# Attention values with 256 moving columns: the parity of the key block picks the column half of the array, and the two partial sums are added afterwards

## The chip, the cores and the metric

One Trainium2 chip, one of its cores. The metric is the device time of one execution in microseconds (us); the median of three executions of the kernel before is 1148.51 us.

## The reference, cut to what matters

One layer of a transformer trunk for 640 tokens (128 context tokens and 512 latent tokens), width 1024: a norm with modulation, a combined projection, grouped attention beside a short gated convolution, a merge, and a feed-forward part. The change lies in the last step of the attention, the product of the probabilities with the values:

```python
def one_block(qblk):
    s = jnp.einsum('bqkgd,btkd->bkgqt', qblk, k).astype(jnp.float32) * scale
    p = jax.nn.softmax(s, axis=-1).astype(v.dtype)
    return jnp.einsum('bkgqt,btkd->bqkgd', p, v)
```

There are 16 query heads of 64 columns and 4 heads of keys and values, so four query heads share one head of keys and values; call these four a **group** g (0 to 3). Latent queries see 640 keys (512 latent, 128 cached), context queries see the 128 context keys. All data are 32-bit floats.

## The kernel before, in words

The program has three long stages: a prologue with the projections of keys and values, the attention (about 75 to 298 us of the profiled span), and then a row of large products that run to the end. The first product after the attention is the attention's output projection.

**Attention.** For each group there are nine **steps**, i = 0 to 8. Step 0 treats the context queries; steps 1 to 8 treat one block of 128 latent queries and a pair of heads each. TensorE, ScalarE and VectorE run in exactly the order in which the code is written (a manual schedule); GpSimd's order is chosen by the scheduler. In one step:

- TensorE computes scores into two PSUM tiles `s` of a pool of three (12 matmuls, line 603). A score tile can be overwritten when the exponentials of the scores that it held are done.
- In steps 0, 3, 4, 5 and 8 TensorE also transposes a block of queries into the PSUM bank S1[1] (`s1b` in the profile, line 584), and multiplies a later block of queries into S1[0] (`s1a`, 24 matmuls of 256 columns at lines 161 to 163). In group 3, which has no next group, 24 matmuls of a gate (`gate_part`) into S1[0] stand there in steps 3, 4, 5 and 8. In steps 0, 1, 4 and 6 there are 32 small matmuls of the modulation (line 214).
- VectorE takes two row maxima (line 739), ScalarE makes the scale of each (741) and the exponentials with their sums (742), VectorE the reciprocal of the sums (745), GpSimd multiplies the probabilities by it, one head at a time (750), and VectorE transposes the result in 32 by 32 blocks into one of six slots of the SBUF tile PT (755), one step later. ScalarE and VectorE also make the high and low halves of a weight (700, 701) in steps 1 and 6, and VectorE and GpSimd rotate and scale the queries (538 to 558).

**The values** (class `Values`). PT holds transposed probabilities in blocks of 32 keys. A matmul takes 32 partitions of PT (one of four 32-row strips i, which are different queries) as moving data, and a block of 32 keys by 64 value columns as weights, so eight such matmuls work in eight tiles of the array at a time: four row strips by two column halves of 64. Before the change the column half is the head h of the pair: the same weights stand in both halves, and each half sees the 128 columns (4 slots by 32 queries) of its own head. Twenty key blocks are accumulated. Strip i writes to its own PSUM bank: strips 0 and 1 to the two banks of a tile `s`, strips 2 and 3 to S1[0] and S1[1]. Each 32-bit matmul appears as two matmuls and two weight loads in the profile.

One group needs two such sums, the **halves**: half 0 (three query blocks, the context block among them, which `own` adds with four key blocks) is spread over steps 6 and 7, half 1 (two query blocks) over steps 1 and 2 of the next group, and for group 3 after its last step. When the last matmul of a half is done, at the end of step 7 or 2, ScalarE copies the sums to the high tensor AH (three activations, line 796), and VectorE subtracts this from the sums into the low tensor AL (three instructions, line 800). Only then are S1[0], S1[1] and the tile `s` free: the transposition of queries in step 8 or 3 waits for S1[1], the query or gate product behind it for S1[0].

**The end of the attention.** After step 8 of group 3 TensorE runs 18 matmuls of 384 columns for a gate (`gate1`), four small ones that fold the modulation (line 240); VectorE finishes the modulation (244 to 247) and transposes the last probabilities (755); then the last half runs, with 6 more gate matmuls in it, and when its sums have been read from S1[0] and S1[1], the projection starts in banks `b` that take the place of S1.

Tile names in the profile: `s`, `s1a`, `s1b` are the PSUM tiles above, `AL`, `KH`, `KL` hold value blocks when they are inputs of line 783 (they are reused as room for the values of a group), `CT` the transposed context probabilities.

## Time and profile before

| | us |
|---|---|
| three executions | 1143.9, 1148.51, 1150.22 |
| the profiled execution's own time | 1150.66 |
| its span, first to last instruction | 1148.9 |
| attention from group 0's step 6 to group 3's step 6 | 152.38 |
| from there to the first matmul of the projection | 39.01 |
| matmuls in the program, as profiled | 10013 |

The span is what all views of the profile share out; the profiled execution's own time is 1.8 us longer, and lies 2.15 us above the median. In the profile "PE" is TensorE's matmuls, "PEld" its weight loads, DVE is VectorE, ACT is ScalarE, POOL is GpSimd. Each row of a timeline starts with the start and the duration in us; a bracket at the row's end says how long the engine sat idle before it, and what ended that. "issue" means that nothing the profile shows was waited for. In a table of windows, a row gives the window, its length, then for each engine its busy time and in parentheses its instructions, then the share of TensorE's clock that was granted.

### The profile page before, as it was taken

To read this page: it belongs to the slowest core of one execution; us is meant where nothing else is said; L and a number is where in the kernel's file an instruction comes from. 1 tells how busy PE (TensorE), PEld (TensorE's weight loads), DVE (VectorE), ACT (ScalarE), POOL (GpSimd) and SP (SyncE) were. 2 spreads that over 40 slices of the span, in tenths; PEclk is the share of its full clock that TensorE was granted. 3 is DMA by queue.
4 is the path that set the end of the run, shared out by engine and by line. 5 is a ranking of instruction groups with operands and counts; after the bars stand their busy time and mean duration, and the time that the engine had idled before them with its cause. 6 is when DMAs were issued, how large, how long until landed. Compare 5 with 4: busy or idle time off the path is not lost.

```text
span 1148.9 us, 23748 instructions
## 1 busy us (share of the span) xinstructions
PE 1100.1 (96%) x10013; PEld 1020.2 (89%) x10013; DVE 819.5 (71%) x1194; ACT 555.4 (48%) x999; POOL 162.2 (14%) x198
## 2 busy tenths in 40 slices
PE   7998888897999999999999999999999999999997
PEld 5787777787999999999999888999999999998786
DVE  5578777885454788898745447887887778888644
ACT  4375555564233545454532347555545455555431
POOL 2057564663000000000000012000000000002001
PEclk9998999998899999999999999999999999999999
DMA  9664336341122233233242543333333233315632
GB/s 336 205 171 148 113 94 140 94 130 57 45 70 73 74 97 88 74 94 90 74 127 75 185 165 126 92 115 101 103 115 96 93 102 106 113 60 184 229 106 91
DMA packets 189000, 133.65 MB, mean 116 GB/s; under 512 B 16914, under 2 KB 171086, under 8 KB 188878
## 3 DMA queue, kind: packets, MB, share of 16 engines
q1 hardware_dynamic: 188782, 132.11, 37.3%
q8 instruction: 78, 1.28, 0.5%
q14 instruction: 28, 0.23, 0.1%
q10 hardware_dynamic: 112, 0.04, 0.0%
HBM read 120.01 MB, written 12.24 MB: 115 GB/s over the span
## 4 chain that ended last, share of the span: by engine, by line
PE 90%; DVE 3%; issue 3%; DMA 2%; ACT 1%; SPq 1%; POOL 0%; DVEq 0%; POOLq 0%; ACTq 0%
PE b L1011 44%; PE b L163 9%; PE b L161 9%; PE b L162 9%; PE s L603 3%; PE s L783 3%; PE s1a L161 2%; PE s1a L162 2%; PE s1a L163 2%; DVE Y L1495 1%; PE s L161 1%; PE s1a L783 1%; PE s L163 1%; DMA XT<-in_w_ada_dram 1%; PE s L162 1%
## 5 line engine op out<-in xcount | busy, mean ns | idle before, releaser
L1011 PE MATMUL b<-ZB,whi 128*128 128x322 f32 x1024 | 228.6, 310 | 0.0
L1011 PEld LDWEIGHTS b<-ZB,whi 128*128 128x128 f32 x1024 | 173.8, 189 | 1.6
L1011 PE MATMUL b<-ZB,wlo 128*128 128x322 f32 x512 | 159.5, 311 | 0.0
L1011 PE MATMUL b<-MT,whi 128*128 128x320 f32 x608 | 134.2, 308 | 0.0
L1011 PEld LDWEIGHTS b<-MT,whi 128*128 128x128 f32 x608 | 101.6, 188 | 0.0
L1011 PEld LDWEIGHTS b<-ZB,wlo 128*128 128x128 f32 x512 | 96.3, 188 | 0.0
L750 POOL TENSOR_TENSOR pr<-pr,sm 128x640 f32<-128x640 f32 x64 | 86.7, 1375 | 57.7 <-DVE sm L745 56.9
L1011 PE MATMUL b<-MT,wlo 128*128 128x320 f32 x304 | 93.8, 309 | 0.0
L1495 DVE SCALAR_TENSOR_TENSOR Y<-C,cffn,Y 128x642 f32<-128x642 f32 x88 | 80.8, 920 | 0.9
L998 ACT ACTIVATE whi<-SUM 128x1024 fp32r<-128x1024 f32 x40 | 42.2, 1056 | 79.6 <-DVE SUM L1465 77.2
L136 DVE TENSOR_TENSOR wlo<-raw,whi 128x1024 fp32r<-128x1024 f32 (+1 forms) x31 | 33.7, 1086 | 52.6 <-ACT whi L135 52.1
L1011 PE MATMUL b<-UH,whi 128*128 128x320 f32 x228 | 70.6, 310 | 0.0
L1011 PE MATMUL b<-UL,whi 128*128 128x320 f32 x228 | 70.5, 309 | 0.0
L1011 PE MATMUL b<-UH,wlo 128*128 128x320 f32 x228 | 70.3, 308 | 0.0
L1002 DVE TENSOR_TENSOR wlo<-raw,whi 128x1024 fp32r<-128x1024 f32 (+1 forms) x51 | 50.4, 1020 | 25.2 <-ACT whi L998 24.4
L998 ACT ACTIVATE whi<-WB 128x1024 fp32r<-128x1024 f32 x38 | 40.1, 1055 | 54.9 <-DVE WB L1106 54.9
L1019 ACT ACTIVATE p<-b 128x322 f32<-128x322 f32 (+1 forms) x78 | 34.2, 439 | 58.3 <-PE b L1011 58.3
L742 ACT ACTIVATE pr<-s,mr,rq 128x640 f32<-128x640 f32 x64 | 56.6, 885 | 3.8
L1011 PEld LDWEIGHTS b<-MT,wlo 128*128 128x128 f32 x304 | 57.0, 188 | 0.0
L1022 DVE TENSOR_TENSOR C<-b,p 128x322 f32<-128x322 f32 x40 | 19.7, 492 | 52.3 <-PE b L1011 51.8
L739 DVE TENSOR_REDUCE mx<-s 128x1 f32<-128x640 f32 x64 | 49.6, 816 | 8.7 <-PE s L603 8.2
L1002 DVE TENSOR_TENSOR wlo<-WB,whi 128x1024 fp32r<-128x1024 f32 x38 | 46.5, 1223 | 8.5 <-ACT whi L998 8.5
(379 smaller groups left out, 3151.9 us busy)
## 6 DMA issues: line engine op xcount, KB each, us to landing
raw<-in_w_in_dram SPq DMA_DIRECT2D x48, 512.0 KB, 3.6
RAW<-in_w_up_dram SPq DMA_DIRECT2D x40, 512.0 KB, 3.9
raw<-in_w_ada_dram SPq DMA_DIRECT2D x32, 512.0 KB, 4.6
raw<-in_w_down_dram SPq DMA_DIRECT2D x22, 512.0 KB, 3.8
actd<-Y SPq DMA_DIRECT2D x18, 321.0 KB, 2.6
AFB<-actd SPq DMA_DIRECT2D x18, 321.0 KB, 4.5
XT<-in_w_ada_dram SPq DMA_DIRECT2D x9, 512.0 KB, 5.7
raw<-in_w_conv_out_dram SPq DMA_DIRECT2D x9, 512.0 KB, 4.1
```

What stands on the lines that cost most here:

```text
L161: PE.matmul(out, ah, bh, start=start, stop=False)
L162: PE.matmul(out, ah, bl, start=False, stop=False)
L163: PE.matmul(out, al, bh, start=False, stop=stop)
L603: PE.matmul(outs[h], q[rows, pi, :], kk[rows, g, ks], start=n == 0, stop=n == 2, tile_position=(64 * h, 0))
L739: V.tensor_reduce(out=mx, in_=self.sc[h], axis=AX.X, op=ALU.max, negate=True)
L742: S.activation(self.pr[:, h, :], self.sc[h], AF.Exp, bias=low, scale=rs, accum_out=self.sm[:, h:h + 1])
L750: G.tensor_tensor(out=self.pr[:, h, :], in0=self.pr[:, h, :], in1=self.sm[:, h:h + 1].broadcast_to((128, NTOK)), op=ALU.mult)
L783: PE.matmul(self.out(i, h, 64, 192), VR[self.g][rows, c, :], PT[rows, s0:s0 + 4, h, 32 * c:32 * c + 32], start=c == 0, stop=c == 19, tile_ ...
L998: S.activation(to[0], raw, AF.Copy)
L1002: V.tensor_tensor(out=lo, in0=raw, in1=hi.bitcast(F32), op=ALU.subtract)
L1011: PE.matmul(out, p[:, ws], q[:, k, :], start=start and k == 0 and n == 0, stop=stop and k == 3 and n == 2, skip_group_check=True)
L1495: V.scalar_tensor_tensor(out=y, in0=crows(j)[i][:, d:d + NACT], scalar=cffn[:, 44 * d + o:44 * d + o + 1], in1=y, op0=ALU.mult, op1=ALU.add)
```

## The change

The roles of the two column halves change. Both halves now see the same kind of moving data, the 256 columns of both heads (4 slots by 2 heads by 32 queries), and the half is picked by the parity of the key block: even blocks accumulate in PSUM partitions 0 to 63, odd blocks in partitions 64 to 127. Each half of a group takes ten pairs of blocks, and `own` two, so there are half as many matmuls (and weight loads) with twice the columns. What leaves the array are two partial sums that have to be added. The new method `sums` does this: ScalarE copies the odd partial sums from PSUM to SBUF (three activations, into slots of PT that have been used up), and VectorE adds even and odd in eight instructions over 64 partitions, and writes the complete sums into another part of these slots, head 0 to partitions 0 to 63 and head 1 to 64 to 127. `high` is then one activation from SBUF, and `low` one instruction, on GpSimd, except for the last half, where it is on VectorE. The output of a strip now takes 384 of the 512 columns of a bank (before 192), so the modulation's results in S1[1] move from columns 256 to 383 to columns 384 to 511. What each step computes, and the order of the steps, stay as they are; the parts of a half are divided alike (3 and 7 pairs for 6 and 14 blocks, 5 and 5 for 10 and 10; 3, 3, 4 pairs for 7, 7, 6 blocks at the end).

```diff
-                        for h in range(2):
-                            PE.matmul(self.out(i, h, 64, 192), VR[self.g][rows, c, :], PT[rows, s0:s0 + 4, h, 32 * c:32 * c + 32],
-                                      start=c == 0, stop=c == 19, tile_position=(32 * i, 64 * h))
+                        for c in (2 * n, 2 * n + 1):
+                            PE.matmul(self.out(i, c % 2, 128, 384), VR[self.g][rows, c, :], PT[rows, s0:s0 + 4, :, 32 * c:32 * c + 32],
+                                      start=n == 0, stop=n == 9, tile_position=(32 * i, 64 * (c % 2)))
...
+            def sums(self):
+                a, q = (128, 2) if self.half else (0, 3)
+                w, s0 = 384 - a, 4 if self.half else 0
+                room = PT[:, s0:s0 + 2].rearrange("p s h c -> p (s h c)")
+                odd = room[0:64, 0:4 * w].rearrange("p (i c) -> p i c", i=4)
+                self.all = room[:, 4 * w:6 * w].rearrange("p (k c) -> p k c", k=2)
+                dst = self.all.rearrange("p k (q i b) -> p i q k b", q=q, i=4)
+                both = self.p.rearrange("p (e c) -> p e c", e=2)[:, :, a:384]
+                for i in (1, 0):
+                    S.activation(odd[:, 2 + i], S1[i][64:128, a:384], AF.Copy)
+                S.activation(odd[:, 0:2], both[64:128], AF.Copy)
+                one, two = "p (q k h b) -> p h q k b", "p e (q k h b) -> p h q k e b"
+                for h in range(2):
+                    rows = slice(64 * h, 64 * h + 64)
+                    for i in (1, 0):
+                        x, y = (z.rearrange(one, h=2, k=2, b=32)[:, h] for z in (S1[i][0:64, a:384], odd[:, 2 + i]))
+                        V.tensor_tensor(out=dst[rows, 2 + i], in0=x, in1=y, op=ALU.add)
+                    for k in range(2):
+                        x, y = (z.rearrange(two, h=2, k=2, b=32)[:, h, :, k] for z in (both[0:64], odd[:, 0:2]))
+                        V.tensor_tensor(out=dst[rows, 0:2, :, k].rearrange("p e q b -> p q e b"), in0=x, in1=y, op=ALU.add)
...
             def high(self):
-                for src, (hi, lo) in self.views():
-                    S.activation(hi, src, AF.Copy)
-
-            def low(self):
-                for src, (hi, lo) in self.views():
-                    V.tensor_tensor(out=lo, in0=src, in1=hi.bitcast(F32), op=ALU.subtract)
+                _, (hi, lo) = self.ends()
+                S.activation(hi, self.all, AF.Copy)
+
+            def low(self, eng=G):
+                _, (hi, lo) = self.ends()
+                eng.tensor_tensor(out=lo, in0=self.all, in1=hi.bitcast(F32), op=ALU.subtract)
...
                 if out:
+                    out.sums()
                     out.high()
                 st.shares()
                 if out:
                     if keep:
                         keep()
                     out.low()
```

At three places the order of an engine's instructions shows what moved. First TensorE in step 6 of group 0, where four blocks of the values stand before the scores of step 7 (`s` with a number is the PSUM tile of strips 0 and 1; a shape like 64x128 is output partitions by moving columns). Before:

```order
L783 MATMUL s_215_1419<-PT,AL 64x128 x4
L783 MATMUL s1a<-PT,AL 64x128 x2
L783 MATMUL s1b<-PT,AL 64x128 x2
L783 MATMUL s_215_1419<-PT,AL 64x128 x4
L783 MATMUL s1a<-PT,AL 64x128 x2
L783 MATMUL s1b<-PT,AL 64x128 x2
L783 MATMUL s_215_1419<-PT,AL 64x128 x4
L783 MATMUL s1a<-PT,AL 64x128 x2
L783 MATMUL s1b<-PT,AL 64x128 x2
L783 MATMUL s_215_1419<-PT,AL 64x128 x4
L783 MATMUL s1a<-PT,AL 64x128 x2
L783 MATMUL s1b<-PT,AL 64x128 x2
```

Now the same four blocks:

```order
L782 MATMUL s_215_1419<-PT,AL 64x256 x4
L782 MATMUL s1a<-PT,AL 64x256 x2
L782 MATMUL s1b<-PT,AL 64x256 x2
L782 MATMUL s_215_1419<-PT,AL 64x256 x4
L782 MATMUL s1a<-PT,AL 64x256 x2
L782 MATMUL s1b<-PT,AL 64x256 x2
L603 MATMUL s_224_1484<-KH,Q_1173 128x320
```

Sixteen matmuls of 256 columns stand where thirty-two of 128 columns stood.

Second, VectorE in step 7 of group 1, from the maxima of this step to those of step 8 (`mx` is a maximum, `sm` the sums of the exponentials, `tabk` the modulation's accumulator). Before:

```order
L739 TENSOR_REDUCE mx_2589<-s_337_2457 128x1
L755 STREAM_TRANSPOSE PT<-pr_2329 128x1280
L745 RECIPROCAL sm_2471<-sm_2471 128x2
L235 TENSOR_TENSOR tabk<-tabk,s1b 128x128
L800 TENSOR_TENSOR AL<-s1b,AH 128x3x2x32
L800 TENSOR_TENSOR AL<-s1a,AH 128x3x2x32
L800 TENSOR_TENSOR AL<-s_327_2351,AH 128x3x2x64
L739 TENSOR_REDUCE mx_2625<-s_344_2605 128x1
```

Now:

```order
L739 TENSOR_REDUCE mx_2331<-s_337_2255 128x1
L755 STREAM_TRANSPOSE PT<-pr_2167 128x1280
L805 TENSOR_TENSOR PT<-s1b,PT 64x3x2x32
L805 TENSOR_TENSOR PT<-s1a,PT 64x3x2x32
L808 TENSOR_TENSOR PT<-s_327_2189,PT 64x3x64 x2
L805 TENSOR_TENSOR PT<-s1b,PT 64x3x2x32
L805 TENSOR_TENSOR PT<-s1a,PT 64x3x2x32
L808 TENSOR_TENSOR PT<-s_327_2189,PT 64x3x64 x2
L745 RECIPROCAL sm_2269<-sm_2269 128x2
L235 TENSOR_TENSOR tabk<-tabk,s1b 128x128
L739 TENSOR_REDUCE mx_2374<-s_344_2354 128x1
```

Eight additions stand where there were three subtractions, and they now stand ahead of the reciprocal of the step, not behind it; S1[1] (`s1b`) is read last by the fifth of them, S1[0] by the sixth.

Third, ScalarE in step 7 of group 0 (`pr` are the probabilities, `mr` the scaled maximum). Before:

```order
L742 ACTIVATE pr_1538,sm_1539<-s_225_1525,mr_1658,rq_684 128x640
L796 ACTIVATE AH<-s1b 128x3x2x32
L796 ACTIVATE AH<-s1a 128x3x2x32
L796 ACTIVATE AH<-s_215_1419 128x3x2x64
L587 ACTIVATE Q_1691<-s1b 128x256
```

Now:

```order
L742 ACTIVATE pr_1498,sm_1499<-s_225_1485,mr_1562,rq_684 128x640
L798 ACTIVATE PT<-s1b 64x384
L798 ACTIVATE PT<-s1a 64x384
L799 ACTIVATE PT<-s_215_1419 64x768
L812 ACTIVATE AH<-PT 128x2x384
L587 ACTIVATE Q_1602<-s1b 128x256
```

The copies stand behind the exponentials of step 7, as the activations before did; the new activation for AH waits for VectorE's last addition, and the copy of the transposed queries (587) is queued behind it.

More of the change, by code (lines that the diff above doesn't have):

```diff
@@ L772, in own @@
                         rows = slice(32 * i, 32 * i + 32)
-                        for h in range(2):
-                            PE.matmul(self.out(i, h, 0, 64), VC[rows, j, self.g * HD:(self.g + 1) * HD], ct[rows, h, j], start=j == 0,
-                                      stop=j == 3, tile_position=(32 * i, 64 * h))
-            def part(self, blocks):
+                        PE.matmul(self.out(i, j % 2, 0, 128), VC[rows, j, self.g * HD:(self.g + 1) * HD], ct[rows, j], start=j < 2,
+                                  stop=j >= 2, tile_position=(32 * i, 64 * (j % 2)))
@@ L964, in trunk_layer @@
         for n in range(3):
-            v.part(range(7 * n, min(7 * n + 7, 20)))
+            v.part(((0, 1, 2), (3, 4, 5), (6, 7, 8, 9))[n])
             if n < 2:
                 gate1_part(range(6 + n, 7 + n))
+        v.sums()
         v.high()
-        v.low()
+        v.low(V)
     atts.close()
```

29 lines of the change are left out of this document (13 added, 16 removed).

## Prediction

> **What bounds the kernel now.** I read the page first: its totals, its chain, and its queues.
>
> ```profile
> PE 90%; DVE 3%; issue 3%; DMA 2%; ACT 1%; SPq 1%; POOL 0%; DVEq 0%; POOLq 0%; ACTq 0%
> q8 instruction: 78, 1.28, 0.5%
> ```
>
> TensorE carries 90% of the chain that ends last, so time on it counts. But 3% of the chain is "issue": TensorE stands still and waits for nothing that the profile shows. The second line is a queue that fetches instructions: 78 packets and 1.28 MB, 16.4 KB each. The program has 10013 matmuls and as many weight loads, 20026 instructions, which is 257 for each packet: this queue is TensorE's, and a packet is a page of 256 instructions.
>
> Next the view of waits, for TensorE between 100 and 300 us, which is the attention.
>
> ```profile
> PE s1a L783 <- issue: 10.6, 6, 3.0
> PE s L783 <- issue: 9.8, 5, 2.7
> PE s L783 <- DVE PT L755: 2.7, 1, 2.7
> ```
>
> Nearly all "issue" stands at line 783, the matmuls that are changed: 20.4 us in 11 stalls. Where they lie is seen in windows that run from the end of one stall to the end of the next (first three rows; matmuls in parentheses), and in the two rows of TensorE's timeline where the last two of these windows end.
>
> ```profile
> 111.57:115.29 3.72, 3.27 (x128) 1.00 0.46 139
> 115.30:120.39 5.09, 2.09 (x128) 1.00 0.35 104
> 165.56:170.37 4.81, 2.09 (x128) 1.00 0.41 112
> ...
> 120.40 0.33 PE L783 MATMUL s1a<-PT,AL 32*64 32x128 f32 x2 [3.01 <-issue]
> 170.38 0.42 PE L783 MATMUL s<-PT,AL 32*64 32x128 f32 x3 [2.74 <-issue]
> ```
>
> From stall to stall there are exactly 128 matmuls, with their weight loads 256 instructions: one page. So TensorE stalls at page borders, because it has used up 256 instructions before the next page is there. A page takes 3.7 to 5.1 us here. TensorE runs through 128 of these matmuls much faster than that:
>
> ```profile
> 185.80:188.30 2.50, 2.43 (x160) 1.00 0.80 229
> ```
>
> 160 of them, from the first start (185.87) to the next scores (188.14 is the last start), take 2.27 us, 14.2 ns each, so a page lasts 1.8 us. (A rule of the Trainium skill speaks against this: the page "Runtime: NRT & Kernel Launch", section "Instruction fetch mechanics", has fetches of 16 KiB blocks hidden, because instructions are issued more slowly than they arrive. The block size agrees with 16.4 KB; that the fetch is hidden does not, by the rows above.)
>
> A stall also costs afterwards, though not each (none behind the one that ended at 120.40, first row). Four stretches of 3.4 us in the loop (three of them below) and two at its end have half the clock:
>
> ```profile
> 120.40:125.20 4.80, 4.75 (x47) 1.00 0.02 5
> 139.80:143.20 3.40, 3.40 (x114) 0.50 0.40 114
> 170.50:173.90 3.40, 3.40 (x74) 0.50 0.02 5
> 218.30:221.70 3.40, 3.40 (x77) 0.50 0.57 159
> 272.90:283.10 10.20, 10.20 (x48) 0.50 0.00 0
> 286.60:293.40 6.80, 5.99 (x171) 0.50 0.01 2
> ```
>
> Each begins during or soon after a time in which TensorE stood still for some 2 us or more (the one at 170.50 right behind the stall of 2.74 us that ended at 170.38; the last in the wait of 2.7 us for PT). The expensive one is 272.9 to 283.1, where TensorE works without a gap at half speed.
>
> **The change: what goes.** Matmuls and weight loads of the values halve, columns double. At 28.4 ns each (twice 14.2) the stream takes as long as before, 2.27 us for 80, and a page now lasts 128 times 28.4 ns, 3.6 us, without the scores that lie in between (12 matmuls in 1.15 us). Against 3.7 to 5.1 us for a fetch, what is left of a stall is about 1 us at most, and that lies in a wait that I come to now. I cost the fetch at nothing.
>
> **What is late next.** With the stall gone, the next scores must still wait until the exponentials of this step have freed their tiles. Step 7 of group 1, on ScalarE and VectorE:
>
> ```profile
> 161.63 1.05 ACT L700 ACTIVATE whi<-raw 128x1024 fp32r<-128x1024 f32 x1
> 162.71 2.08 DVE L701 TENSOR_TENSOR wlo<-raw,whi 128x1024 fp32r<-128x1024 f32 x1 [0.54 <-ACT whi L700]
> 164.71 1.54 DVE L739 TENSOR_REDUCE mx<-s 128x1 f32<-128x640 f32 x2
> 167.12 0.89 ACT L742 ACTIVATE pr<-s,mr,rq 128x640 f32<-128x640 f32 x1
> ```
>
> The weight's low half delays the maxima, and the second exponential ends at 168.01, 6.52 us after the step's start at 161.49. TensorE would be through at 161.49 + 1.15 + 112 x 0.0284 = 165.8. So of the two stalls in this step some 2.2 us come back as a wait for ScalarE.
>
> **What is added.** Behind the last matmul of a half stood, before, this (ScalarE, VectorE, then TensorE's transposition of queries):
>
> ```profile
> 172.43 0.33 ACT L796 ACTIVATE AH<-s1b 128x192 fp32r<-128x192 f32 x1 [4.33 <-PE s1b L783]
> 172.86 0.50 ACT L796 ACTIVATE AH<-s 128x384 fp32r<-128x384 f32 x1
> 173.00 0.35 DVE L800 TENSOR_TENSOR AL<-s1b,AH 128x192 fp32r<-128x192 f32 x1
> 173.26 0.35 DVE L800 TENSOR_TENSOR AL<-s1a,AH 128x192 fp32r<-128x192 f32 x1
> 173.53 0.55 DVE L800 TENSOR_TENSOR AL<-s,AH 128x384 fp32r<-128x384 f32 x1
> 174.08 0.44 PE L584 MATMUL s1b<-ident,qf 128*128 128x128 f32 x2
> ```
>
> 1.8 us from the values' end (172.28) to 174.08. Now: copies of 384, 384 and 768 columns. 384 columns take 0.50 us and 1024 take 1.05, so 768 take about 0.84 (an estimate between those rows). They start 0.1 us after the exponentials and end at +0.6, +1.0 and +1.7 us. The additions have 192 elements per partition, as line 800 on s1b: 0.35 us, and 0.26 us from start to start. Two run early; the two on `s` start at +1.75, the fifth, on s1b, ends at +2.64, the sixth at +2.9, the eighth at +3.4. No row shows an addition over 64 partitions that moves data to other partitions: its price lies between 0.26 (the start-to-start time) and 0.55 us (twice the elements, line 800 on `s`); I take 0.35, the row of the same size. In half 1 (256, 256, 512 columns; 128 elements) the same sum gives +2.0 us for the fifth. The low half on GpSimd, about 1.5 us by line 750's 1375 ns for 640 columns, stands between two steps' multiplications; nothing waits for AL within the loop.
>
> Queued behind these instructions: on VectorE the step's reciprocal (so GpSimd's multiplications and the transposition to PT), on ScalarE the new activation for AH (0.84 us) and behind it the copy of the queries. VectorE has no room to catch up:
>
> ```profile
> 106.47:258.85 152.38, 132.60 (x3209) 116.46 (x3209) 119.16 (x207) 84.81 (x221) 92.24 (x90) 0.96 0.42 115
> 258.85:297.86 39.01, 31.53 (x826) 28.30 (x825) 15.40 (x30) 12.64 (x32) 10.83 (x8) 0.78 0.15 43
> ```
>
> Its 119.16 us (third busy figure) of three groups grow by six times 1.0, to 125. I add 2.0 us for what spills into step 0.
>
> **The sum, loop.** The places concerned before, steps 6 to 8 of three groups, then steps 1 to 3, and single steps without a stall:
>
> ```profile
> 106.47:125.20 18.73, 14.13 (x480) 1.00 0.31 88
> 157.15:177.31 20.16, 15.59 (x479) 0.92 0.40 105
> 210.85:229.03 18.18, 15.08 (x479) 0.91 0.32 90
> 130.45:147.12 16.67, 14.60 (x415) 0.90 0.41 123
> 182.56:200.82 18.26, 14.89 (x415) 0.91 0.47 135
> 234.29:249.27 14.98, 12.92 (x415) 1.00 0.47 137
> ...
> 157.15:161.49 4.34, 4.34 (x205) 3.78 (x204) 3.82 (x8) 2.65 (x7) 3.90 (x5) 1.00 0.27 79
> 234.29:238.93 4.64, 4.64 (x205) 4.08 (x204) 3.34 (x9) 2.87 (x8) 3.72 (x6) 1.00 0.67 197
> ...
> 243.97 0.88 ACT L742 ACTIVATE pr<-s,mr,rq 128x640 f32<-128x640 f32 x1
> ```
>
> Half 0 after: step 6 4.34, then 6.52 to the exponentials' end, 2.64 to the transposition, and 3.23 from there to the next step (177.31 - 174.08): 16.73. Three times this is 50.2, against 57.07: 6.9 us gained. Half 1 after: step 1 4.64, 5.92 to the exponentials' end (238.93 to 244.85), 2.0, 3.23: 15.8, three times 47.4 against 49.91: 2.5 gained. With the 2.0 lost, 7.4. But TensorE now stands still for 2 us and more before the scores of steps 8 and 3, as long as what halved the clock before; a stretch of 3.4 us at half clock loses 1.7 us of work. I expect two that count in the loop: 3.4. **Loop: 4.0 us gained.**
>
> **The sum, end.** Before 39.01 us (row above). After, from group 3's step 6: 4.34, then 6.2 (between 5.92 and 6.52) to the exponentials, 10.5. S1[0] is free 2.9 later, and `gate`, `gate1` and the fold then take some 5 us. They are not the longest: the maxima of step 8 start only behind the additions, its exponentials end 7.1 us after those of step 7, at 17.6, and reciprocal, GpSimd's two multiplications and the transposition add 0.2, 2.5 and 1.5: 21.8. The values take 160 x 28.4 ns = 4.5, six gate matmuls 1.0, the copies and six additions 2.2 us: 29.5. Gained: 9.5, less 1.7 for one stretch of half clock here, and 1.7 for one at the projection's start, where TensorE waits 2.2 us: **6.1 us**.
>
> Together 10.1 us. Against the profiled execution's 1150.66 that is 1140.6; it lies 2.15 above the median, so on the median **1138.4 us**.
>
> **Rivals.** Differences under 0.5% (5.7 us) this kernel's measurement hardly tells from none.
>
> - *The clock never drops.* For it: the waits that are left are shorter than the longest stalls, and the one of 3.01 us had no half clock behind it. Against: four of the stalls in the loop did. It gives back 6.8 us: 1131.6. (By a rule of the Trainium skill, page "TensorE: Matmul & The Clock Gate", section "Part 1: The HAM clock gate (the "warmup" mystery)", the clock is halved only after a whole idle window of about 3.4 us, and that would make this case certain. The trace disagrees: a stall of 2.74 us was enough.)
> - *The clock drops behind all seven waits*, and again at the projection's start: eight times 1.7, 6.8 more than I took, 1145.2. For it: the waits come in every group; against: only four of the eleven stalls in the loop were answered so.
> - *The additions cost more: slower.* 64 additions stand on VectorE, which is nearly full. At 0.51 us each instead of 0.35 they eat the 10.1 us; at 0.60 the kernel is slower by 0.5%, at 0.7 by 12.3 us (1160.8). For it: half the lanes, other partitions, PSUM and SBUF read together. Against: line 800 reads PSUM and SBUF together, and takes 0.35.
> - *The change does not do what it says:* the stalls are not the fetch, and stay, so that only the chain's growth is left, (2.64 - 1.8) x 8, 6.7 us: 1155.2. Against it are the 128 matmuls from stall to stall. (The Trainium skill's sentence on hidden fetches would make this one true.)
>
> **How the numbers follow.** Forecast 0.47 (1133 to 1143), no half clock 0.17, half clock everywhere 0.20, additions dear 0.11, stalls stay 0.05. Additions at 0.26 without half clock would give 1125.8, at 0.55 1151.2; the range 1128 to 1152 leaves out most of the last two cases and little else. Faster by over 0.5% (below 1142.8) are the first two, less a little, 0.62; slower the last two, less a little, 0.14; the rest 0.24.
>
> **What would show it.** In the profile after: line 782 with 1280 matmuls and "issue" before it of a few us instead of 20; scores of steps 8 and 3 that wait for ScalarE (line 742) 2 us and more; line 584 waiting for VectorE (line 805) some 1.5 us behind the scores; additions of 0.35 us; the end (39.01) at 30 to 33 us, the loop (152.38) at 145 to 150. Wrong would be: additions of 0.5 us or more, matmuls of 256 columns at more than 30 ns each, stalls of 2 us at line 782, or half clock for as long as before.

## The result and the profile after

| | before | after |
|---|---|---|
| median of the executions, us | 1147.59 | 1161.02 |
| lowest and highest, us | 1143.9 to 1150.22 | 1160.17 to 1162.69 |
| span of the profiled execution, us | 1148.9 | 1159.2 |
| attention, group 0's step 6 to group 3's step 6, us | 152.38 | 162.66 |
| from there to the first matmul of the projection, us | 39.01 | 37.83 |

The changed kernel takes 1.0121 times as long, with a 95% interval of 1.0090 to 1.0152: it is slower by about 14 us, where 10 us less were forecast. (The median before is that of four executions, the three listed under the time before and one of 1146.67 us.)

First the chain of work that ended last, and the queue that fetches instructions, from the page of the changed kernel:

```profile
PE 84%; DVE 6%; ACT 3%; POOL 3%; issue 2%; DMA 1%; DVEq 0%; POOLq 0%; SPq 0%; ACTq 0%
q8 instruction: 67, 1.10, 0.4%
```

Against the rows of before, TensorE has lost six points of the chain and VectorE has gained three; the queue moved 67 pages for 78. TensorE is no longer held up by its instructions but by the engines behind the values. What it waits for between 100 and 320 us (total us, times, longest):

```profile
PE s L603 <- ACT pr L742: 12.8, 14, 1.4
PE s1b L584 <- DVE tabk L235: 12.7, 6, 2.7
```

The 20.4 us of "issue" at the values' line are gone. In their place stand 12.8 us in which scores wait for the exponentials, and 12.7 us in which the transposition of queries into S1[1] (line 584) waits, not for the additions (lines 805, 808) but for line 235. That is the keep: the addition with which VectorE takes the modulation's result out of S1[1].

The windows of the changed kernel (times, length, busy time of TensorE, its weight loads, VectorE, ScalarE and GpSimd, then the granted clock): the loop, the end, steps 6 to 8 of group 1, steps 1 to 3 of group 2, and some stretches at the clock's own borders.

```profile
106.25:268.91 162.66, 138.18 (x2153) 117.34 (x2152) 123.82 (x237) 91.61 (x227) 101.44 (x97) 0.87 0.39 107
268.91:306.74 37.83, 29.33 (x474) 23.94 (x473) 18.04 (x40) 14.59 (x32) 12.58 (x9) 0.82 0.15 43
160.34:180.59 20.25, 15.83 (x287) 13.24 (x286) 15.63 (x29) 11.39 (x26) 14.51 (x14) 0.83 0.67 144
185.85:204.77 18.92, 15.16 (x256) 12.51 (x256) 13.74 (x27) 10.67 (x25) 11.49 (x12) 0.82 0.36 109
...
169.89:173.30 3.41, 1.55 (x12) 1.07 (x12) 2.06 (x5) 2.94 (x8) 0.18 (x1) 1.00 0.44 127
173.30:180.13 6.83, 4.91 (x23) 4.94 (x24) 5.09 (x12) 3.55 (x8) 5.10 (x4) 0.50 1.17 191
...
197.20:204.02 6.82, 5.24 (x28) 4.86 (x25) 5.36 (x15) 3.80 (x9) 4.18 (x4) 0.50 0.01 2
...
282.53:292.77 10.24, 10.02 (x39) 10.05 (x40) 3.98 (x9) 5.03 (x10) 6.67 (x5) 0.50 0.01 2
```

The loop's clock is 0.87 (0.96 before). Behind every one of its six halves stand 6.8 us at half clock, as in the rows from 173.30 and 197.20; before there were four stretches of 3.4 us in the whole loop. In the 3.41 us ahead of the row from 173.30, TensorE worked for 1.55 us only. The rest is not one long stall but pieces of three waits (0.27, 0.78 and 0.81 us); the third piece is the beginning of the wait of 2.72 us shown next.

How the waits come about is seen in the timeline of the end of step 7 of group 1 (start, duration; in brackets the idle time before, and what ended it). The last four rows are the same for half 1, which ends in step 2 of group 2.

```profile
170.16 0.41 PE L603 MATMUL s<-KH,Q 64*128 64x320 f32 x1 [0.77 <-ACT pr L742]
170.32 0.88 ACT L742 ACTIVATE pr<-s,mr,rq 128x640 f32<-128x640 f32 x1
...
171.35 0.41 PE L603 MATMUL s<-KH,Q 64*128 64x320 f32 x1 [0.78 <-ACT pr L742]
...
173.55 0.35 DVE L805 TENSOR_TENSOR PT<-s1b,PT 64x192 f32<-64x192 f32 x1
...
174.81 0.27 DVE L235 TENSOR_TENSOR tabk<-tabk,s1b 128x128 f32<-128x128 f32 x1
...
175.22 0.66 PE L584 MATMUL s1b<-ident,qf 128*128 128x128 f32 x2 [2.72 <-DVE tabk L235]
...
180.59 0.33 PE L603 MATMUL s<-KCH,Q 64*128 64x128 f32 x2
...
195.53 0.88 ACT L742 ACTIVATE pr<-s,mr,rq 128x640 f32<-128x640 f32 x1
...
199.19 0.27 DVE L235 TENSOR_TENSOR tabk<-tabk,s1b 128x128 f32<-128x128 f32 x1
...
199.60 0.66 PE L584 MATMUL s1b<-ident,qf 128*128 128x128 f32 x2 [1.58 <-DVE tabk L235]
...
204.77 0.41 PE L603 MATMUL s<-KH,Q 64*128 64x320 f32 x2
```

The fifth addition, the last one that reads S1[1], ends at 173.90. The transposition starts 1.32 us later, right behind the keep (in half 1 it is 1.12 us). From the transposition to the next step are 5.37 us, where there were 3.23 before.

### The profile page after: what moved, and what is told of

Its sections match the earlier page's. It is cut to its first block, busy times and chain, and to the rows that moved or that the text cites. A ratio compares the mean times of both kernels' runs of the same rounds, so it can differ in the third digit from the quotient of the medians.

```text
span 1159.2 us, 21001 instructions
## 1 busy us (share of the span) xinstructions
PE 1105.9 (95%) x8605; PEld 1019.1 (88%) x8605; DVE 827.6 (71%) x1235; ACT 564.6 (49%) x1007; POOL 173.2 (15%) x205
## 4 chain that ended last, share of the span: by engine, by line
PE 84%; DVE 6%; ACT 3%; POOL 3%; issue 2%; DMA 1%; DVEq 0%; POOLq 0%; SPq 0%; ACTq 0%
PE b L1029 44%; PE b L161 9%; PE b L163 9%; PE b L162 9%; POOL pr L750 3%; PE s1a L161 2%; PE s1a L162 2%; PE s1a L163 2%; PE s L603 2%; ACT pr L742 1%; DVE Y L1513 1%; DVE PT L755 1%; PE s L161 1%; PE s L163 1%; DVE mx L739 1%
## 5 line engine op out<-in xcount | busy, mean ns | idle before, releaser
L603 PE MATMUL s<-KH,Q 64*128 64x320 f32 x256 | 44.5, 343 | 18.2 <-ACT pr L742 17.6
L603 PEld LDWEIGHTS s<-KH,Q 64*128 64x128 f32 x256 | 29.8, 191 | 29.5 <-ACT pr L742 24.3
```

What stands on the lines that cost most here:

```text
L603: PE.matmul(outs[h], q[rows, pi, :], kk[rows, g, ks], start=n == 0, stop=n == 2, tile_position=(64 * h, 0))
```

## The experiments

The theory after the result, called **A**: the stalls at the page borders are gone as forecast, and the loss has three parts behind the values. (1) S1[1] comes free with the keep, 1.1 to 1.3 us behind the fifth addition. (2) The scores of steps 8 and 3 wait for exponentials that the weight's low half (line 701, VectorE) delays. (3) These waits together halve TensorE's clock for two windows behind each half. Rivals: **B**, the additions and copies themselves set the time, wherever the keep stands; **C**, the clock is only a symptom. Every ratio is against runs of the kernel before on the same chip; the loop and its clock are those of the profiled execution. For the kernel before they are 152.38 us and 0.96; its profiled execution was one of its longer ones (1150.66 us, median 1147.59), and that of "before, low half later" one of the shorter (1139.67 us, median 1144.53), so that their loops differ by more than their ratios do.

| kernel | ratio, 95% interval | loop, us | its clock |
|---|---|---|---|
| changed | 1.0121 (1.0090 to 1.0152) | 162.66 | 0.87 |
| keep first | 1.0049 (1.0025 to 1.0073) | 153.76 | 0.92 |
| keep first, S1 first | 0.9986 (0.9963 to 1.0008) | 150.08 | 0.92 |
| changed, waits filled | 1.0032 (1.0007 to 1.0057) | 157.39 | 0.92 |
| changed, no sums | 0.9901 (0.9867 to 0.9934) | 143.89 | 0.94 |
| keep and S1 first, low half later | 0.9944 (0.9928 to 0.9961) | 145.40 | 0.98 |
| before, low half later | 0.9982 (0.9957 to 1.0008) | 146.06 | 0.96 |
| changed, 128 columns | 1.0209 (1.0175 to 1.0242) | 166.62 | 0.93 |
| changed, low half later | 0.9961 (0.9940 to 0.9982) | 147.09 | 0.94 |
| **keep and S1 first, low half on GpSimd** | **0.9851 (0.9830 to 0.9872)** | 140.73 | 0.99 |
| the same, transposition between | 0.9978 (0.9957 to 0.9998) | 151.37 | 0.97 |
| before, low half on GpSimd | 0.9957 (0.9927 to 0.9986) | 145.82 | 0.98 |
| no sums, low half on GpSimd | 0.9786 (0.9734 to 0.9837) | 134.10 | 0.99 |

### 1. The keep ahead of the additions

```diff
                 if out:
+                    if keep:
+                        keep()
                     out.sums()
                     out.high()
                 st.shares()
                 if out:
-                    if keep:
-                        keep()
                     out.low()
```

> The modulation's keep (an addition of VectorE that reads columns 384 to 511 of S1[1]) is moved ahead of the eight additions; nothing else. Theory A: S1[1] is released by its last reader, the keep, 1.3 us behind the fifth addition, and TensorE's waits there, with those for the exponentials, halve its clock for two windows of 3.41 us in each half. Then the transposition of queries starts 1.3 us sooner in six of the seven halves, only one of the two windows is halved, and each such place becomes about 2 us shorter: 1161 - 12 = 1149 us (1146 to 1152). Rival B: the eight additions are what TensorE waits for, whichever of them reads S1[1]: no change, 1159 to 1162. Rival C: the wait gets shorter but the clock is halved as long as now: 6 x 1.3 = 8 us, 1153.

Measured: 1150.33 us, ratio 1.0049, some 8 us less than the changed kernel. The timeline at the end of step 7 of group 1:

```profile
167.34 0.24 DVE L235 TENSOR_TENSOR tabk<-tabk,s1b 128x128 f32<-128x128 f32 x1
...
170.08 0.35 DVE L805 TENSOR_TENSOR PT<-s1b,PT 64x192 f32<-64x192 f32 x1
...
170.58 0.41 PE L584 MATMUL s1b<-ident,qf 128*128 128x128 f32 x2 [1.55 <-DVE PT L805]
```

and its waits:

```profile
PE s1b L584 <- DVE PT L805: 6.8, 6, 1.6
```

The transposition now starts 0.15 us behind the fifth addition, and its wait is 1.55 us for 2.72. Rival B is out: which instruction reads S1[1] last matters, although the keep reads other columns than the transposition writes. The loop is 8.9 us shorter for six waits that are 5.9 us shorter in all (12.7 to 6.8), so the clock gave something as well (0.92 for 0.87; seven windows of half clock are left in the loop, of twelve).

### 2. The additions on S1 first

```diff
-                for h in range(2):
-                    rows = slice(64 * h, 64 * h + 64)
-                    for i in (1, 0):
+                for i in (1, 0):
+                    for h in range(2):
+                        rows = slice(64 * h, 64 * h + 64)
                         x, y = (z.rearrange(one, h=2, k=2, b=32)[:, h] for z in (S1[i][0:64, a:384], odd[:, 2 + i]))
                         V.tensor_tensor(out=dst[rows, 2 + i], in0=x, in1=y, op=ALU.add)
+                for h in range(2):
+                    rows = slice(64 * h, 64 * h + 64)
                     for k in range(2):
```

> As the kernel with the keep first, and the eight additions stand in another order: the two that read S1[1], the two that read S1[0], then the four on the s tile. Theory A: S1[1] and S1[0] are then read by the time the scores of step 8 or 3 are done, the waits of 2.7 us go, and no window is halved behind half 0; the end section keeps its full clock in its 42 matmuls as well. About 3.3 us in each of six halves and 6 us at the end: 1161 - 20 - 6 = 1135 us (1130 to 1142). Rival B: VectorE's whole time is the limit, in whatever order: as the kernel with the keep first, within 3 us of it. Rival C (the clock falls because TensorE waits for the exponentials, not for S1): half clock as long as in the kernel with the keep first, and 1143 to 1149.

Measured: 1143.1 us, ratio 0.9986; about 7 us less than with the keep first, and 8 us more than A gave. The waits of TensorE:

```profile
PE s L603 <- ACT pr L742: 12.5, 14, 1.4
...
PE s1b L584 <- DVE PT L805: 0.4, 2, 0.2
```

The waits for S1[1] are gone (0.4 us of 12.7). What A had wrong is the clock. The waits for the exponentials are as long as they were, and alone they still halve one window of 3.41 us at each of the six places, at one of them two, seven in all as in experiment 1: the loop's clock stays at 0.92. That is rival C of this run, as to the clock.

### 3. The waits filled

```diff
+                    self.spare = both[1][:, 0:128]
...
+                if i == 8 or i == 3 and g:
+                    for n in range(10 if i == 8 else 3):
+                        PE.matmul(st.spare, ident, ident, start=True, stop=True)
                 low = q_turn(*turn, S1[1]) if turn else None
```

> The changed kernel as it is, but TensorE gets 10 matmuls of 128 by 128 (step 8) and 3 (step 3) into unused columns of a score tile, behind the scores, where it waits for S1[1]. They compute nothing that is used. No wait of the program becomes shorter. Theory A (half clock is a large part of the loss): the window behind half 0 is no longer halved, the first one behind half 1 still is, because the wait for the exponentials alone is 2.2 us of 3.4; about 1.9 us less at three places, 1.7 at three, 5 at the end: 1161 - 16 = 1145 us (1142 to 1150). Rival (the clock is a symptom, the chain of copies and additions sets the time): 1159 to 1164, since every transposition of queries starts when it did.

Measured: 1149.24 us, ratio 1.0032, some 10 us less than the changed kernel although TensorE does more and nothing else does less. The timeline behind step 7 of group 1 (line 907 is the filling), and the window from a border of the clock to the next step:

```profile
172.44 2.50 PE L907 MATMUL s<-ident 128*128 128x128 f32 x20
...
175.24 0.41 PE L584 MATMUL s1b<-ident,qf 128*128 128x128 f32 x2 [0.30 <-DVE tabk L235]
...
178.44 0.33 PE L603 MATMUL s<-KCH,Q 64*128 64x128 f32 x2
```

```profile
173.71:178.44 4.73, 4.43 (x39) 4.14 (x37) 4.03 (x10) 3.47 (x8) 3.39 (x3) 1.00 1.32 196
```

The transposition stands where it stood (175.24 and 175.22), but from there to the next step are 3.20 us instead of 5.37, at full clock. Behind step 7 of groups 0 and 2 the same stretch takes 3.17 us (5.16 and 5.45 in the changed kernel). The half clock is a cost of its own, not a symptom. Of what the edit brings, 5.3 us lie in the loop and 5.5 us in the end:

```profile
264.12:296.44 32.32, 26.06 (x493) 21.00 (x493) 18.24 (x40) 14.49 (x32) 12.61 (x9) 1.00 0.18 51
```

Here the end runs at full clock, in 32.32 us for 37.83. In the loop the half clock did not go everywhere: behind step 7 of groups 0 and 2, and behind each half 1, the waits for the exponentials still halved one window or two.

### 4. No sums

Behind the values of 256 columns stand the activations and subtractions of the kernel before.

```diff
-                    out.sums()
                     out.high()
...
+                for src, (hi, lo) in self.views():
+                    S.activation(hi, src, AF.Copy)
```

> The partial sums are not added: behind the values of 256 columns stand the three activations and three subtractions of the kernel before, on as many columns of the PSUM tiles as there (this leaves part of the computation out). It shows what half the instructions bring if the sum costs nothing. Theory A: the waits for S1[1] go, the waits for the exponentials (1.5 us in step 8, 2.2 in step 3) stay, half clock stays behind half 1 alone: 4.7 us less than the changed kernel at three places, 2.5 at three, 10 at the end: 1161 - 31 = 1130 us (1124 to 1137), well under the kernel before. Rival (the stalls that went have only made room for waits for the exponentials, and these halve the clock as well): 1143 to 1150, as the kernel before.

Measured: 1132.96 us, ratio 0.9901. A's time is right within 3 us. One wait of TensorE is left in the loop:

```profile
PE s L603 <- ACT pr L742: 12.6, 14, 1.4
```

It still halves windows (clock 0.94), as in experiment 2. A's account of the clock did not hold: one window is halved behind half 0 of each of the three groups, where A had none, and behind only two of the three halves 1; that the two errors cancel is luck. So half the instructions bring some 11 us against the kernel before if the sum costs nothing, and the sum as written costs 25 us (ratio 1.0121 to 0.9901), more than twice what is gained.

### 5, 6 and 8. The weight's low half behind the maxima

In step 7 or 2 the subtraction for a weight's low half stood ahead of the two maxima. Three kernels move it behind them: the one of experiment 2, the kernel before, and the changed kernel.

```diff
             S.activation(hi, raw, AF.Copy)
-            V.tensor_tensor(out=lo, in0=raw, in1=hi.bitcast(F32), op=ALU.subtract)
             state["cut"].append(Unit((hi, lo), units[i][4]))
-            ring_used(1)
+            def rest():
+                V.tensor_tensor(out=lo, in0=raw, in1=hi.bitcast(F32), op=ALU.subtract)
+                ring_used(1)
+            cut_rest.append(rest)
...
+                while cut_rest:
+                    cut_rest.pop(0)()
                 last.turned()
```

> The kernel with the keep first and the additions on S1 first, and in addition the subtraction that makes the low half of a weight (2.0 us on VectorE, ahead of the two maxima of step 7 or 2) is moved behind these maxima. Theory A (what is left of the loss is the 12.5 us in which TensorE waits for the exponentials of steps 7 and 2, and the half clock that these waits bring): the exponentials end about 4.5 us after the step's start instead of 6.8, the waits for them fall to under 3 us, and nearly all half clock in the loop goes: about 3 us less at three places, 2.5 at three, 1 to 2 at the end, 1143 - 18 = 1125 us (1119 to 1133). Rival B (VectorE is full, so the subtraction only moves in front of the additions, and TensorE waits for S1 instead): 1138 to 1146.

> The kernel before, with the subtraction that makes the low half of a weight moved behind the maxima of step 7 or 2, and nothing else. Theory A: there the values stand still at the page borders until the exponentials are long done, so that nothing waits for them: no change, 1145 plus or minus 4 us. Rival: the exponentials are late there too, and the kernel before gains 8 us or more; then what this edit brings is no part of the change.

> The changed kernel with the subtraction for the weight's low half moved behind the maxima, and nothing else: keep and additions stay as they are. Theory A (both waits count, those for the exponentials and those for S1[1]): the waits for the exponentials fall from 12.8 us to under 4, the waits for S1[1] grow from 2.7 to some 3.3 us because the subtraction and the transposition now stand ahead of the additions, and about 2.5 us go at each of six places: 1145 us (1140 to 1152). Rival B (S1[1] alone decides: what the exponentials lose is won again before S1[1] is free): 1157 to 1163.

Measured: 1138.37 (0.9944), 1144.53 (0.9982) and 1140.85 us (0.9961). The waits of the first:

```profile
PE s1b L584 <- DVE PT L808: 4.7, 3, 1.6
...
PE s1a L161 <- DVE PT L808: 3.7, 7, 2.1
PE s1b L584 <- ACT PT L802: 2.9, 3, 1.0
...
PE s L603 <- ACT pr L745: 2.2, 3, 0.7
```

and of the changed kernel with this edit alone:

```profile
PE s1b L584 <- DVE tabk L235: 13.9, 6, 2.7
...
PE s L603 <- ACT pr L745: 2.0, 3, 0.7
```

In both the waits for the exponentials fall from 12.5 us and more to about 2. In the changed kernel that alone is worth 18 us (ratio 1.0121 to 0.9961): the largest single item. The waits for S1[1] did not shrink there (nor grow to 3.3 us, as A had it), they only came earlier. The gains do not add up: the edits of experiment 2 bring 15 us, this one 18, and both together 20 (0.9944). In the kernel before the same edit does nothing that can be told from no change, because there the page stalls cover it: no wait for the exponentials stands among its waits, and 17.7 us of stalls at the page borders do. The first of the three fell short of A by 13 us and ended where its rival B had it: with the subtraction behind the maxima, VectorE comes to the additions later, and TensorE waits for S1 again, 11.3 us in the three kinds of rows for lines 808 and 802.

### 7. Matmuls of 128 columns again

```diff
-                            PE.matmul(self.out(i, c % 2, 128, 384), VR[self.g][rows, c, :], PT[rows, s0:s0 + 4, :, 32 * c:32 * c + 32],
-                                      start=n == 0, stop=n == 9, tile_position=(32 * i, 64 * (c % 2)))
+                            for s in range(2):
+                                PE.matmul(self.out(i, c % 2, 128 + 128 * s, 256 + 128 * s), VR[self.g][rows, c, :],
+                                          PT[rows, s0 + 2 * s:s0 + 2 * s + 2, :, 32 * c:32 * c + 32],
+                                          start=n == 0 and s == 0, stop=n == 9 and s == 1,
+                                          tile_position=(32 * i, 64 * (c % 2)))
```

> The changed kernel with each matmul of 256 columns written as two of 128 columns, with the same weights: as many matmuls and weight loads of the values as in the kernel before, the sums as changed. Theory A (the stalls were instruction pages): about 20 us of stalls for which the profile shows no cause come back at the values' line, 128 matmuls apart, the waits for the exponentials (12.8 us) shrink to a few us, and the time is 1161 + 20 - 10 = 1171 us (1165 to 1178). Rival (the stalls came from something else that the change removed, such as two heads in two halves of the array): no such stalls, 1158 to 1164.

Measured: 1168.11 us, ratio 1.0209, 10 us above the changed kernel. Its waits, and a window from the end of one stall to the end of the next:

```profile
PE s L783 <- issue: 4.6, 4, 1.8
PE s1b L783 <- issue: 4.1, 4, 1.5
...
PE s L603 <- issue: 2.3, 2, 1.4
PE s1a L783 <- issue: 2.0, 1, 2.0
```

```profile
223.68:228.20 4.52, 2.79 (x128) 2.55 (x128) 1.85 (x2) 2.16 (x6) 1.05 (x2) 1.00 0.41 120
```

Eleven stalls without a cause in the profile are back, 13.0 us of them, in the window above 128 matmuls apart, with the data, the column halves and the sums of the change. The stalls belong to the number of instructions. That they are waits for pages can be read from the traces as well: each of these eleven stalls ends 1.34 to 1.50 us behind the end of a packet of 16384 bytes of the queue that fetches TensorE's instructions, and each of twelve in the kernel before (the eleven at line 783 and one at line 603) 1.19 to 1.50 us; the stall that ended at 120.40, for one, had its packet from 118.00 to 118.93. The prediction's reading of them is shown. They are 13 us and not 20.

### 9 and 10. The low half on GpSimd

To the kernel of experiment 2, in `cut_hi`; the second kernel also puts VectorE's transposition of the step before between the additions on S1 and those on `s`.

```diff
-            V.tensor_tensor(out=lo, in0=raw, in1=hi.bitcast(F32), op=ALU.subtract)
+            G.tensor_tensor(out=lo, in0=raw, in1=hi.bitcast(F32), op=ALU.subtract)
```

> The kernel with the keep first and the additions on S1 first, and in it the subtraction for the low half of a weight is made by GpSimd, not by VectorE. Theory A (with the subtraction only moved behind the maxima, VectorE's whole work in steps 7, 8 and 0 was the limit; that is why 1138 us came out and not 1125): VectorE loses 2.0 us of work at each of seven places, the exponentials are as early as with the subtraction moved, and TensorE's waits for S1 shrink by about 1.5 us each: 1138 - 10 = 1128 us (1122 to 1134). Rival (GpSimd's multiplications come 2.4 us later, so that the transpositions of the probabilities hold up VectorE instead): 1136 to 1144.

> As the kernel with the subtraction on GpSimd, and VectorE's transposition of the probabilities of the step before (1.5 us) stands between the four additions on S1 and the four on the s tile, no longer ahead of all eight. Theory A: S1 is free about 0.6 us sooner, since VectorE else waits for ScalarE's copies behind the transposition: 2 to 4 us less than with the subtraction on GpSimd. Rival (the s tile and the maxima of the next step come later by as much, and TensorE waits there): no change, or slower by up to 4 us.

Measured: 1129.66 us, ratio 0.9851, and 1144.46 us, ratio 0.9978. The first beats both kernels, by 1.5% the kernel before. Its waits and its loop:

```profile
PE s1a L161 <- ACT sq L550: 6.9, 8, 1.5
...
PE s L603 <- ACT pr L742: 2.1, 3, 0.7
PE s1b L584 <- DVE PT L805: 2.0, 3, 0.7
```

```profile
106.52:247.25 140.73, 128.28 (x2154) 106.67 (x2154) 115.37 (x232) 91.28 (x226) 109.62 (x103) 0.99 0.45 123
```

The waits for the exponentials and for S1[1] are both small at last, and the loop's clock is 0.99. What is left is another wait, the first row: the next product into S1[0] waits for ScalarE to read the query product before (line 550); the longest, 1.49 us, stands ahead of the only window of half clock in this loop. VectorE's 115.37 us against 123.63 with the subtraction only moved (and GpSimd's 109.62 against 98.49) fit A: VectorE's load held experiment 5 back. The second kernel is 15 us slower than the first. Its timeline at the end of step 7 of group 1, then that of the first kernel:

```profile
166.89 0.29 DVE L235 TENSOR_TENSOR tabk<-tabk,s1b 128x128 f32<-128x128 f32 x1 [2.45 <-PE s1b L782]
...
169.22 1.51 DVE L755 STREAM_TRANSPOSE PT<-pr 128x1280 f32<-128x1280 f32 x1
...
171.98 1.54 DVE L739 TENSOR_REDUCE mx<-s 128x1 f32<-128x640 f32 x2
```

```profile
161.31 1.51 DVE L755 STREAM_TRANSPOSE PT<-pr 128x1280 f32<-128x1280 f32 x1 [0.61 <-POOL pr L750]
...
166.40 1.53 DVE L739 TENSOR_REDUCE mx<-s 128x1 f32<-128x640 f32 x2
```

The scores of step 8 start at 166.71 in the second kernel and at 162.39 in the first, so the maxima of step 8 stand 5.27 us behind them instead of 4.01. In the first kernel the transposition of probabilities ran while VectorE had nothing to do but wait for the last matmul of the values. Moved between the additions, it left that time empty (2.45 us of waiting ahead of the keep), S1[1] came free only 0.1 us sooner (the transposition of queries 1.88 us behind the scores' start instead of 2.02), and everything behind it on VectorE came 1.3 us later. The rival had the mechanism, but not the size: it was put at up to 4 us. How the 15 us divide among the places is not shown.

### 11 and 12. What is the change's own

The same edit, subtraction on GpSimd, in the kernel before and in the kernel without sums.

> The kernel before, with the subtraction for the low half of a weight made by GpSimd, and nothing else: whether the 1130 us of the kernel with this edit, the keep first and the additions on S1 first need the values of 256 columns at all. Theory A: the kernel before stands still at the page borders, so freeing 2.0 us of VectorE at seven places brings nothing: 1145 plus or minus 4 us. Rival: it gains 8 us or more, and the values of 256 columns have less part in the 1130.

> The kernel whose partial sums are not added (which leaves part of the computation out), with the subtraction for the low half of a weight on GpSimd as well: against the 1130 us of the kernel that adds them, with keep and S1 first and the subtraction on GpSimd, it gives the price of the sum once its surroundings are in order. Theory A: the sum still costs its waits for S1 and for what is queued behind it on VectorE, about 1.5 us at each of seven places: 1119 us (1114 to 1124). Rival: the sum is hidden by now: 1126 to 1131.

Measured: 1140.61 us, ratio 0.9957 (0.9927 to 0.9986), and 1121.69 us, ratio 0.9786 (0.9734 to 0.9837). The waits of the kernel before with the edit:

```profile
PE s1a L783 <- issue: 7.6, 5, 2.6
PE s L783 <- issue: 7.5, 5, 2.2
```

The page stalls are still there (these rows are the largest two), and the edit is worth 5 us, neither nothing (A) nor the 8 us and more of the rival. So of the 17 us by which the kernel of experiment 9 is ahead of the kernel before, 5 would come without the change; the other 12, by the two intervals give or take 4, come with the values of 256 columns. Against the kernel without sums, experiment 9 still pays some 8 us for the sum, about 1 us at each of the seven places and no longer 3.6; the two intervals leave this open by 6 us either way, so that it is smaller than the 25 us, but its size is not settled.

## Why the prediction was wrong, point by point

- **The stalls are instruction pages: right.** They went with half of the instructions and came back with them, and each ends behind a packet of the queue that fetches them (experiment 7).
- **The stream takes no longer: right.** Step 6 of group 1 takes 4.09 us (160.34 to 164.43) where 4.34 were put, step 1 of group 2 4.43 for 4.64.
- **What is late next: right.** The exponentials of step 7 end at 171.20, 10.86 us after the start of step 6, as in the sum (4.34 + 6.52); those of step 2 end 10.56 us after the start of step 1, as in the sum. The waits are 1.55 us in step 8 and up to 2.2 in step 3, where some 2.2 were put. What was left out is that this wait can be taken away at almost no cost: moving one subtraction is worth 18 us (experiment 8).
- **What the additions cost: right as to each, wrong as to what it sets free.** An addition of 192 elements takes 0.35 us, and the fifth ends 2.70 us behind the exponentials (2.64 put). The step that failed is the next one: "the fifth, on s1b, ends at +2.64" was taken for the release of S1[1]. The keep (line 235) reads S1[1] too, the change had put it behind all eight additions and the reciprocal, as VectorE's order ahead of the prediction shows, and the transposition starts 4.02 us behind the exponentials; in half 1 it is 3.19 us, where 2.0 were put. That is 1.4 and 1.2 us, about 7.7 us if each counts at three places. Experiment 1 shows the wait go with the keep.
- **The clock: the step that cost most.** "I expect two that count in the loop", 3.4 us. There are twelve windows of half clock, two behind each half. From the transposition to the next step there are 5.03 to 5.45 us at the six places instead of 3.23, 12.0 us in all, 8.6 more than allowed for. Experiment 3 shows that behind half 0 this comes back at full clock. The error was to look for single stalls of 2 us, as in the trace of before: pieces of three waits, none over 0.81 us, in one window did it as well. The second window follows one at half clock in which TensorE still stood waiting for the keep; without that wait seven windows are left of twelve (experiment 1).
- **The backlog of 2.0 us in step 0: wrong.** Step 0 takes 5.26 us (180.59 to 185.85), as before (5.25). That VectorE catches up while TensorE runs at half clock is likely, but not shown.
- **The end: wrong by the clock too.** With one stretch of half clock it was put at 31.2 us, and is 37.83. The 42 gate matmuls start at 282.75, 13.8 us behind step 6 where the sum has 13.4, but run until 293.3 at half clock (the row of 282.53 to 292.77) instead of some 5 us, and become the longest path in place of the exponentials: GpSimd has the last probabilities ready at 290.15, but their transposition stands on VectorE behind the modulation, which waits for the fold behind the gate. At full clock the end takes 32.32 us (experiment 3), so the clock costs 5.5 us, 3.8 more than the 1.7 allowed for. The other 2.8 us stand there too: the values start 23.5 us behind step 6, by this queue on VectorE, where 21.8 were put, and from there to the projection 8.8 us pass, where 7.7 were put.
- **The rivals.** "The clock drops behind all seven waits" had the mechanism and a chance of 0.20, but one window for each wait: 1145.2. "Additions dear" is out at 0.35 us, "the stalls stay" is out. The count of four in "the eleven stalls in the loop" was too favourable: two of the eleven lie in the end.

The balance of the misses, in us against the forecast: S1[1] released late 7.7, half clock in the loop 8.6, end 6.6, backlog -2.0, projection and start together -0.5: 20.4, where the span was forecast 10.1 shorter and came out 10.3 longer, a miss of 20.4. That it closes so well is in part chance, since the 7.7 us are read at one place of each kind. The clock's share is shown by experiment 3 for the three places behind half 0 and for the end; behind half 1 it is read from the trace alone.

## What to carry to other kernels

When a stall goes, list for each buffer that the next work needs every reader and where each stands in its engine's queue: the last reader sets it free, and here that was an addition of 0.27 us for something else, pushed back by the new work. Then add up all idle time of TensorE in the stretch, not the longest stall. And an instruction that nobody waited for beside a stall (here a 2 us subtraction ahead of the maxima) becomes the bound when the stall is gone, so look for an engine with less work for it before judging the change.

## What the runs showed of the hardware that was not expected

- **Short waits halve the clock.** TensorE worked 1.55 us of the window from 169.89 to 173.30, in pieces, and the next two were at half clock. In experiment 2 the window from 167.20 to 170.61, with 2.01 us of work and no wait over 0.78 us, was followed by half clock too. The Trainium skill, page "TensorE: Matmul & The Clock Gate", section "Part 1: The HAM clock gate (the "warmup" mystery)", asks for a whole idle window of some 3.4 us, which no window of the changed kernel's attention was; its section "A second HAM failure mode: psum-queue depth-cycling" tells of short idle times that make the clock swing, and with that the trace agrees. What decides is not settled. Idle time alone does not: in the kernel before, three windows in a row at the same place were

```profile
163.68:167.09 3.41, 1.57 (x110) 1.53 (x114) 3.41 (x4) 1.45 (x4) 3.19 (x3) 1.00 0.30 72
167.09:170.50 3.41, 0.67 (x48) 0.43 (x41) 0.74 (x2) 0.98 (x3) 2.12 (x2) 1.00 0.29 88
170.50:173.91 3.41, 3.41 (x74) 3.02 (x73) 1.12 (x4) 0.94 (x3) 0.34 (x1) 0.50 0.02 5
```

  and the one with 1.57 us of work was followed by a window at full clock, the one with 0.67 by one at half.
- **A busy window can stay at half clock.** From 282.53 to 292.77 TensorE was busy for 10.02 of 10.24 us, three windows, and all had a clock of 0.50.
- **A reader of other columns holds the bank.** The transposition writes columns 0 to 255 of S1[1], the keep reads 384 to 511, and the wait was there until the keep was moved (experiment 1). Whether the chip would need this wait was not tried.
